# The first stage of an encoder layer, reordered: the first pair of row tiles, the first transform's cosine blocks, and the last tile's latents

## The chip, the cores and the metric

The kernel runs on one core of one Trainium2 chip. The metric is the device time of one execution in microseconds (us). Each version is run several times, and the median of the runs is its time.

## The reference

Two sequences (x_prompt and x_sample) of 1024 rows by 1024 columns in fp32 go through one layer, each with its own conditioning vector c:

```
mod = silu(c) @ w_ada + b_ada                     # six vectors of 1024
h   = rmsnorm(x, g_mix) * (1 + sc1) + sh1
z   = h @ w_in                                    # 256 q | 128 kv | 64 k_pe | 512 f_in
y_mla  = mla_group(z[q], z[kv], z[k_pe], ...)     # 4 heads, latents rms-normed, rotary k_pe
y_four = real(fft2(f_in, over rows and within 8 groups of 64 columns)) @ w_four
x = x + ga1 * (concat(y_mla, y_four) @ w_out)
h2 = rmsnorm(x, g_ffn) * (1 + sc2) + sh2
x = x + ga2 * ((silu(h2 @ w_gate) * (h2 @ w_up)) @ w_down)
return rmsnorm(x, g_final)
```

## The kernel before

Every fp32 operand of a large product is split into a high part (a cast on ScalarE) and a low part (a subtraction on VectorE), and each product is three matmuls (high·high, high·low, low·high; `mm3`, lines 78 to 80). The split is `split`, lines 62 and 63.

**Stage 1**, the first 230 us or so, works through eight pairs of row tiles, k = 0 to 7, four pairs for each sequence. A pair is two tiles (u = 0, 1) of 128 rows by 1024 columns; two rows of x that are mirror images in the sequence stand in the two tiles, so that the first Fourier product can use their sum ("even") and difference ("odd"). For a pair there is:

- `x_load(k)`: two transfers of 512 KB into the tiles `xt`, of which there are four, issued from SyncE (SP).
- `norm(k)`: the squares of each row on ScalarE (L354, tile `junk`), the reciprocal root on GpSimd (`rstd`, six small operations L101 to L108), and the scaling of both `xt` tiles in place on VectorE (L357). The reciprocal root is taken for both tiles together.
- `flip(k, g)`, g = 0 to 3: transposes of `xt` on TensorE (L370), the modulation on ScalarE (`hf`, L377), the split into `hh` and `hl`.
- `evenodd(k)`: GpSimd adds and subtracts the halves of `hf` (`eo`, L392), and each result is split into `eoh` and `eol`.
- `zproj(k, u)`: 24 matmuls 448 wide; then squares (L406, L407) on ScalarE, `rstd` on GpSimd, rotary products (L413 to L415, tile `t`) and their sum (L417, GpSimd), the scaled latents `lat` (L418, L419) on VectorE, the split `kv`, and its two stores to `ckv_d` (L424) from SP.
- `latents(k, u)`: four transposes of `lat` (L433), the split into `lh` and `ll`, two stores to `lat_d` (L438).
- `fourier_in(k, i)`: 24 matmuls with the even (i = 0, 280 wide) or odd (i = 1, 256 wide) half against the constant `wcs`, and the copy out (L448).

Beside the pairs a generator `extras()` is advanced three times in each pair. It computes the modulation vectors ga1 and ga2 with eight chunks of w_ada (two loads of 512 KB each into `wada`, of which there are two; L202), one chunk a step with four matmuls (L211), and then combines them with w_out in four groups (L299, stores `wm_d` and `wn_d`).

After stage 1, `dft(0)` applies the transform over the rows to the first sequence: per block q, a product with the cosines (`pe`, operand `zh`) and one with the rest (`po`; for its first chunk the operand is `zod`). Then follow the folding of weights, the output of the Fourier part, the second sequence, attention, the output projection and the FFN.

The order of the work is set by a scheduler that takes the program order as priority and its own estimates as times; `issue_after` and `first` add dependencies that only fix an order. Each engine then executes its list strictly in order. SP has one list: a transfer that waits for its data holds back every transfer behind it.

Of the kernel before, what the change touches and what calls it, by code (L numbers as in the profile page):

```python
# [21 lines left out]
P = 128  # L22
D = 1024
N = 1024
NC = D // P
# [27 lines left out]
def hybrid_encoder_kernel(ctx: ExitStack, tc: tile.TileContext, a: dict):  # L53
# [105 lines left out]
    with ExitStack() as st:  # L159
# [36 lines left out]
        def wada_tile():  # L196
            return w2.tile([P, 4, 512], F32, tag="wada", name="wada", bufs=2)
# [67 lines left out]
        def extras():  # L265


            cols1 = [(2 * D, D), (5 * D, D)]
            wt = mod_load(0, cols1, wada_tile())
            yield  # L270
            yield
            wo4 = []
            for c in range(NC):
                if c + 1 < NC:
                    nxt = mod_load(c + 1, cols1, wada_tile())
                else:
# [69 lines left out]
        def norm(k):  # L346
# [6 lines left out]
                jk = w.tile([P, D], BF16, tag="junk", name="junk", bufs=1)  # L353
                nc.scalar.activation(jk, t, AF.Square, scale=1.0 / 32.0, accum_out=ms[:, u : u + 1])  # L354
            r = rstd(ms, 2)
            for u in range(2):
                nc.vector.tensor_scalar(out=xt[u], in0=xt[u], scalar1=r[:, u : u + 1], scalar2=None, op0=ALU.mult)  # L357

        def flip(k, g):
            s, j = pairs[k]  # L360
# [20 lines left out]
        def evenodd(k, root=None):  # L381

            hf = st1.pop(("hf", k))
            eo = []
            for i, op in enumerate((ALU.add, ALU.subtract)):
                f = w.tile([P, NC, P], F32, tag="eo", name="eo", bufs=1)
                fh = w.tile([P, NC, P], F32R, tag=f"eoh{i}", name="eoh", bufs=1)
                fl = w.tile([P, NC, P], F32R, tag=f"eol{i}", name="eol", bufs=1)
                for g in range(2):
                    gs = slice(4 * g, 4 * g + 4)  # L390
                    with tc.issue_after(root) if root is not None and i == 1 else ExitStack():
                        nc.gpsimd.tensor_tensor(out=f[:, gs], in0=hf[:, gs, 0, :], in1=hf[:, gs, 1, :], op=op)  # L392
                    split(fh[:, gs], fl[:, gs], f[:, gs])
                eo.append((fh, fl))
            st1["eo", k] = eo

        def zproj(k, u):
            s, j = pairs[k]
# [3 lines left out]
            for c in range(NC):  # L402
# [4 lines left out]
            nc.scalar.activation(jk[:, QL : QL + KVL], pz[:, QL : QL + KVL], AF.Square, scale=1.0 / math.sqrt(KVL),  # L407
                                 accum_out=mz[:, 1:2])
# [6 lines left out]
            nc.vector.tensor_tensor(out=t1[:, 96:], in0=kp[:, :32], in1=ropes[:, ti, 32:], op=ALU.mult)  # L415
            for d in range(2):
                nc.gpsimd.tensor_tensor(out=sk[:, 384 + 64 * d : 448 + 64 * d], in0=t1[:, :64], in1=t1[:, 64:], op=ALU.add)  # L417
            nc.vector.tensor_scalar(out=sk[:, :QL], in0=pz[:, :QL], scalar1=rz[:, 0:1], scalar2=None, op0=ALU.mult)  # L418
            nc.vector.tensor_scalar(out=sk[:, QL : QL + KVL], in0=pz[:, QL : QL + KVL], scalar1=rz[:, 1:2],  # L419
                                    scalar2=None, op0=ALU.mult)  # L420
# [116 lines left out]
        x_load(2)  # L537
        with behind():
            norm(1)
        norm1 = here["p"]  # L540
        zproj(0, 0)
        evenodd(0, norm1)
        nk = len(pairs)
        more = extras()
# [174 lines left out]
    with ExitStack() as st:  # L719
# [39 lines left out]
        def dft(s):  # L759
            z, od = zh.pop(s)  # L760
            A = [w.tile([P, 2, NT], F32R, tag=f"A{i}", name=f"A{i}", bufs=1) for i in range(2)]
            B = [w.tile([P, 2, 512], F32R, tag=f"B{i}", name=f"B{i}", bufs=1) for i in range(2)]
            for q in (0, 2, 1) if s == 0 else (0, 1):
# [996 lines left out]
```

## Time and profile before

| | |
|---|---|
| runs | 2083.09, 2083.04, 2084.96 us; median 2083.09 us |
| profiled execution | 2080.3 us, of which the span of instructions is 2078.5 us |
| mean granted TensorE clock | 0.996 |
| PE (TensorE matmul) busy | 2025.1 us, 97% of the span |
| VectorE (DVE), ScalarE (ACT), GpSimd (POOL) busy | 1414.6, 902.0, 821.4 us |

The span runs from the first to the last instruction. A row of a timeline gives start, duration, engine, line, operation, the names of output and inputs, the number of instructions that were grouped, and in brackets the idle time of the engine just before and what ended it.

### The profile page before, as it was taken

How to read it: one execution, taken by the hardware profiler on the slowest of the kernel's cores; microseconds unless marked ns; L12 is line 12 of the kernel's file. 1: busy time of each engine (PE TensorE's matmuls, PEld its weight loads, DVE VectorE, ACT ScalarE, POOL GpSimd, SP SyncE). 2: the span in 40 equal slices, each digit the busy share in tenths (PEclk: the TensorE clock that was granted, in tenths of full speed). 3: DMA queues.
4: the chain of work that ended last, by engine and by line, in shares of the span. 5: the costliest groups of instructions: out<-in, count | busy, mean ns of one | idle time of the engine just before them, and what ended most of it. 6: DMA issues, size and time to landing. Idle time of an engine off the chain costs nothing.

```text
span 2078.5 us, 28811 instructions
## 1 busy us (share of the span) xinstructions
PE 2025.1 (97%) x10044; PEld 1659.8 (80%) x10044; DVE 1414.6 (68%) x2085; ACT 902.0 (43%) x1763; POOL 821.4 (40%) x1013
## 2 busy tenths in 40 slices
PE   6899999999999999999999999999999999999998
PEld 3688878888888877888888888877788888888876
DVE  4657757666677667867677666778765666667685
ACT  3666535555565564233323255454323233336441
POOL 0555111111313325878778510333554454420142
PEclk9999999999999999999999999999999999999999
DMA  9675885544644465546446487675322232258662
GB/s 388 217 241 178 270 308 180 134 91 102 167 102 129 146 247 178 191 159 217 170 159 217 147 275 259 213 243 181 120 104 101 96 108 102 87 173 276 229 227 94
DMA packets 185342, 375.49 MB, mean 181 GB/s; under 512 B 18764, under 2 KB 58444, under 8 KB 182124
## 3 DMA queue, kind: packets, MB, share of 16 engines
q1 hardware_dynamic: 167212, 318.06, 45.1%
q0 software_dynamic: 17984, 55.59, 9.0%
q8 instruction: 79, 1.29, 0.3%
q14 instruction: 67, 0.55, 0.1%
HBM read 259.47 MB, written 122.49 MB: 184 GB/s over the span
## 4 chain that ended last, share of the span: by engine, by line
PE 51%; DMA 3%; DVE 3%; issue 1%; POOL 1%; ACT 1%; SPq 1%; DVEq 0%; ACTq 0%; POOLq 0%
PE bank L80 17%; PE bank L79 17%; PE bank L78 17%; DVE wl L63 1%; DMA H<-s_d 1%; DMA val<-x_d 1%; DMA draw<-t_d 1%; DMA draw<-s_d 1%; DVE val L137 1%; POOL val L137 1%; ACT wh L62 0%; DVE val L1566 0%; DMA rgu<-in_wgu_dram 0%; DVE H L63 0%; SPq L1526 0%
## 5 line engine op out<-in xcount | busy, mean ns | idle before, releaser
L80 PE MATMUL bank<-H,wl 128*128 128x512 f32 x1232 | 491.1, 399 | 1.4 <-DVE wl L63 1.4
L78 PE MATMUL bank<-H,wh 128*128 128x512 f32 x1232 | 483.7, 393 | 4.7 <-DVE val L1446 2.1
L79 PE MATMUL bank<-H,wh 128*128 128x512 f32 x1232 | 485.5, 394 | 0.2 <-DVE H L63 0.2
L78 PEld LDWEIGHTS bank<-H,wh 128*128 128x128 f32 x1232 | 231.2, 188 | 61.7 <-DVE val L1446 3.4
L79 PEld LDWEIGHTS bank<-H,wh 128*128 128x128 f32 x1232 | 231.3, 188 | 60.6 <-DVE H L63 0.6
L80 PEld LDWEIGHTS bank<-H,wl 128*128 128x128 f32 x1232 | 231.3, 188 | 55.0 <-DVE wl L63 1.7
L63 DVE TENSOR_TENSOR wl<-draw,wh 128x512 fp32r<-128x512 f32 x286 | 201.2, 737 | 87.4 <-ACT wh L62 87.0
L137 DVE TENSOR_TENSOR val<-bank,val 128x512 f32<-128x512 f32 x200 | 136.6, 689 | 157.3 <-PE bank L80 153.8
L62 ACT CAST wh<-draw 128x512 fp32r<-128x512 f32 x286 | 168.6, 619 | 161.1 <-PE bank L79 82.1
L137 POOL TENSOR_TENSOR val<-val 128x512 f32<-128x512 f32 x58 | 84.2, 1460 | 367.8 <-DVE val L1540 189.3
L79 PE MATMUL bank<-wl,wh 128*128 128x512 f32 x572 | 223.9, 391 | 2.5 <-DVE wl L63 2.5
L78 PE MATMUL bank<-wh 128*128 128x512 f32 x572 | 222.7, 389 | 0.4 <-ACT wh L62 0.4
L80 PE MATMUL bank<-wh,wl 128*128 128x512 f32 x572 | 222.7, 389 | 0.0
L62 ACT CAST wh<-rgu 128x512 fp32r<-128x512 f32 x172 | 106.7, 621 | 266.4 <-PE bank L79 205.8
L62 ACT CAST wh<-val 128x512 fp32r<-128x512 f32 x133 | 82.0, 620 | 276.4 <-PE bank L79 252.8
L63 DVE TENSOR_TENSOR wl<-val,wh 128x512 fp32r<-128x512 f32 x133 | 137.1, 1032 | 82.4 <-ACT wh L62 82.2
L63 DVE TENSOR_TENSOR wl<-rgu,wh 128x512 fp32r<-128x512 f32 x172 | 166.9, 970 | 3.5 <-ACT wh L62 3.4
L134 POOL TENSOR_TENSOR val<-rgu 128x512 f32<-128x512 f32 x80 | 117.4, 1467 | 108.2 <-DMA rgu<-in_wgu_dram 104.5
L79 PEld LDWEIGHTS bank<-wl,wh 128*128 128x128 f32 x572 | 107.3, 188 | 28.4 <-DVE wl L63 6.3
L78 PEld LDWEIGHTS bank<-wh 128*128 128x128 f32 x572 | 107.4, 188 | 23.4 <-ACT wh L62 0.8
L80 PEld LDWEIGHTS bank<-wh,wl 128*128 128x128 f32 x572 | 107.4, 188 | 22.0
L1024 DVE TENSOR_REDUCE mx<-ps_s 128x1 f32<-128x1024 f32 x64 | 78.2, 1222 | 62.0 <-PE ps_s L1019 61.8
(356 smaller groups left out, 4119.1 us busy)
## 6 DMA issues: line engine op xcount, KB each, us to landing
rgu<-in_wgu_dram SPq DMA_DIRECT2D x86, 512.0 KB, 4.2
draw<-s_d SPq DMA_DIRECT2D x143, 256.0 KB, 3.9
s_d<-val POOLq DMA_DIRECT2D x88, 256.0 KB, 3.9
draw<-t_d SPq DMA_DIRECT2D x88, 256.0 KB, 4.3
s_d<-val SPq DMA_DIRECT2D x66, 256.0 KB, 3.6
draw<-in_w_down_dram SPq DMA_DIRECT2D x55, 256.0 KB, 4.6
wada<-in_w_ada_dram SPq DMA_DIRECT2D x11, 1024.0 KB, 8.6
xt<-in_x_dram SPq DMA_DIRECT2D x16, 512.0 KB, 7.8
```

The lines of the kernel that those rows point to most:

```text
L62: here["a"] = nc.scalar.copy(hi, src).ins
L63: here["v"] = nc.vector.tensor_tensor(out=lo, in0=src, in1=rd(hi), op=ALU.subtract).ins
L78: nc.tensor.matmul(out, lh, rh, start=first, stop=False, skip_group_check=cont)
L79: nc.tensor.matmul(out, lh, rl, start=False, stop=False, skip_group_check=cont)
L80: here["t"] = nc.tensor.matmul(out, ll, rh, start=False, stop=last, skip_group_check=cont).ins
L134: return eng.tensor_tensor(out=out, in0=x, in1=y, op=ALU.subtract).ins
L137: eng.tensor_tensor(out=out, in0=x, in1=y, op=ALU.add)
L1024: nc.vector.tensor_reduce(out=mx, in_=ps, axis=AX.X, op=ALU.max)
```

## The change

Four edits:

1. `extras()` loads two chunks of w_ada ahead instead of one, and starts before `zproj(0, 0)`. The product of a chunk comes one step earlier, and so does all that follows it in the generator.
2. In the first pair the rotary products go ahead of the scaling of the second pair's `xt`; the odd half of `evenodd(0)` goes behind the first tile's rotary sum (GpSimd) and its splits behind the second tile's squares; the second tile's scaled latents go behind those splits. On TensorE `fourier_in(0, 1)` goes ahead of `latents(0, 1)`.
3. In the last pair `latents(7, 1)` goes behind the last matmul of `fourier_in(7, 1)`.
4. `dft(0)` does the cosine products of blocks 0 and 1 before any of the other products.

The core of the diff:

```
             cols1 = [(2 * D, D), (5 * D, D)]
-            wt = mod_load(0, cols1, wada_tile())
-            yield
+            ahead = [mod_load(c, cols1, wada_tile()) for c in range(2)]
             yield
             wo4 = []
             for c in range(NC):
-                if c + 1 < NC:
-                    nxt = mod_load(c + 1, cols1, wada_tile())
-                else:
+                mod_mm(1, c, ahead.pop(0))
+                if c + 2 < NC:
+                    ahead.append(mod_load(c + 2, cols1, wada_tile()))
+                elif c + 2 == NC:
...
-                mod_mm(1, c, wt)
-                wt = nxt
                 yield
...
-                    with tc.issue_after(root) if root is not None and i == 1 else ExitStack():
+                    with tc.issue_after(here["root"]) if i == 1 else ExitStack(), tc.issue_after(here["pe"]) if i == 1 and k == 0 else ExitStack():
                         nc.gpsimd.tensor_tensor(out=f[:, gs], in0=hf[:, gs, 0, :], in1=hf[:, gs, 1, :], op=op)
-                    split(fh[:, gs], fl[:, gs], f[:, gs])
+                    with tc.issue_after(here["sq"]) if i == 1 and k == 0 else ExitStack():
+                        split(fh[:, gs], fl[:, gs], f[:, gs])
...
+        scaled = here["xn"]
+        more = extras()
+        next(more)
         zproj(0, 0)
-        evenodd(0, norm1)
+        root0, here["pe"] = here["p"], here["kpe"]
+        for i in scaled:
+            first(here["rope"], i)
+        eo0 = evenodd_steps(0)
+        next(eo0)
         def first_pair():
             zproj(0, 1)
+            here["root"] = root0
+            lats = here["lat"]
+            next(eo0)
+            for i in lats:
+                first(here["v"], i)
             fourier_in(0, 0)
...
-            latents(0, 1)
+            fourier_in(0, 1)
+            with tc.issue_after(here["t"]):
+                latents(0, 1)
             next(more, None)
-            fourier_in(0, 1)
...
             fourier_in(k, 0)
-            latents(k, 1)
+            if k + 1 < nk:
+                latents(k, 1)
             next(more, None)
             fourier_in(k, 1)
+            if k + 1 == nk:
+                with tc.issue_after(here["t"]):
+                    latents(k, 1)
...
+            if s == 0:
+                cosines(0)
+                cosines(1)
             for q in (0, 2, 1) if s == 0 else (0, 1):
...
-                pe, po = bank2(), bank2()
-                for c in range(4):
-                    zz = [(zn[i] if q == 2 else z[0][i][:, :, sl])[:, c, :] for i in range(2)]
-                    mm3(pe[:m, :NTE], zz[0], zz[1], tb[0][0][:, c, :NTE], tb[0][1][:, c, :NTE], c == 0, c == 3)
+                if q not in pes:
+                    cosines(q)
+                pe, po = pes.pop(q), bank2()
```

Line numbers behind the edits shift: L370 becomes L368, L433 becomes L437, L424 becomes L428, L438 becomes L442, L344 becomes L342.

TensorE in the first pair, from the transposes of the second pair's tiles on (L370 or L368), before:

```order
L370 MATMUL bank<-ident,xt 128x128 x8
L433 MATMUL bank<-ident,lat 128x128 x4
L370 MATMUL bank<-ident,xt 128x128 x8
L433 MATMUL bank<-ident,lat 128x128 x4
L211 MATMUL bank<-wada,scT 32x512 x4
L78 MATMUL bank<-wcs_h,eoh 128x256
L79 MATMUL bank<-wcs_l,eoh 128x256
L80 MATMUL bank<-wcs_h,eol 128x256
```

and now:

```order
L368 MATMUL bank<-ident,xt 128x128 x8
L211 MATMUL bank<-wada,scT 32x512 x2
L437 MATMUL bank<-ident,lat 128x128 x4
L368 MATMUL bank<-ident,xt 128x128 x2
L211 MATMUL bank<-wada,scT 32x512 x2
L368 MATMUL bank<-ident,xt 128x128 x6
L78 MATMUL bank<-wcs_h,eoh 128x256
L79 MATMUL bank<-wcs_l,eoh 128x256
L80 MATMUL bank<-wcs_h,eol 128x256
```

A chunk's product (L211) now stands in halves among the transposes of the tiles and inside the odd Fourier product, and the second tile's latents are no longer ahead of that product.

SP's list, around the load of the fourth pair (k = 3: `xt_924` and `xt_925` before, `xt_941` and `xt_942` now). `kv_826` and `kv_907` are the latents of the tiles u = 0 and u = 1 of the second pair (k = 1). Before:

```order
L438 DMA lat_d00_91<-lh_655 512x1x128
L438 DMA lat_d01_92<-ll_656 512x1x128
L438 DMA lat_d00_91<-lh_684 512x1x128
L438 DMA lat_d01_92<-ll_685 512x1x128
L202 DMA wada_690<-in_w_ada_dram 128x1024 x2
L202 DMA wada_835<-in_w_ada_dram 128x1024 x2
L344 DMA xt_924<-in_x0_dram 128x1024
L344 DMA xt_925<-in_x0_dram 128x1024
```

and now:

```order
L202 DMA wada_740<-in_w_ada_dram 128x1024 x2
L428 DMA ckv_d00_95<-kv_826 128x128
L428 DMA ckv_d01_96<-kv_826 128x128
L202 DMA wada_856<-in_w_ada_dram 128x1024 x2
L442 DMA lat_d00_91<-lh_917 512x1x128
L428 DMA ckv_d00_95<-kv_907 128x128
L428 DMA ckv_d01_96<-kv_907 128x128
L442 DMA lat_d01_92<-ll_918 512x1x128
L342 DMA xt_941<-in_x0_dram 128x1024
L342 DMA xt_942<-in_x0_dram 128x1024
```

The load of the fourth pair stood directly behind the chunk loads and ahead of all stores of the second pair; it now stands behind the stores of both tiles of the second pair.

SP's list around the load of the second tile of the last pair (k = 7: `xt_2109` before, `xt_2130` and `xt_2131` now). `kv_1982` and `kv_2022` are the latents of tile u = 0 of the sixth pair (k = 5), `kv_2096` those of its tile u = 1. Before:

```order
L438 DMA lat_d10_93<-lh_1834 512x1x128
L438 DMA lat_d11_94<-ll_1835 512x1x128
L293 DMA gah_1840<-ga_d_81 128x512
L293 DMA gah_1841<-ga_d_81 128x512
L458 DMA zo1_116<-zo_115 1x14x20
L424 DMA ckv_d10_97<-kv_1982 128x128
L424 DMA ckv_d11_98<-kv_1982 128x128
L344 DMA xt_2109<-in_x1_dram 128x1024
```

and now:

```order
L428 DMA ckv_d10_97<-kv_2022 128x128
L428 DMA ckv_d11_98<-kv_2022 128x128
L442 DMA lat_d10_93<-lh_2106 512x1x128
L442 DMA lat_d11_94<-ll_2107 512x1x128
L342 DMA xt_2130<-in_x1_dram 128x1024
L428 DMA ckv_d10_97<-kv_2096 128x128
L428 DMA ckv_d11_98<-kv_2096 128x128
L342 DMA xt_2131<-in_x1_dram 128x1024
L442 DMA lat_d10_93<-lh_2165 512x1x128
```

The second tile's load has gone from behind the stores of tile u = 0 to behind those of tile u = 1 of the same pair. In the same way the load of the second tile of the fifth pair (k = 4) now stands behind the stores of tile u = 1 of the third pair.

More of the change, by code (lines that the diff above doesn't have):

```diff
@@ L355, in norm @@
             r = rstd(ms, 2)
-            for u in range(2):
-                nc.vector.tensor_scalar(out=xt[u], in0=xt[u], scalar1=r[:, u : u + 1], scalar2=None, op0=ALU.mult)
+            here["xn"] = [nc.vector.tensor_scalar(out=xt[u], in0=xt[u], scalar1=r[:, u : u + 1], scalar2=None, op0=ALU.mult).ins
+                          for u in range(2)]
         def flip(k, g):
@@ L379, in flip, with evenodd_steps @@
             split(st1["hh", k][:, gs], st1["hl", k][:, gs], hf[:, gs])
[L381 removed]
+        def evenodd_steps(k):
             hf = st1.pop(("hf", k))
[L384 removed]
+            eo = st1["eo", k] = []
             for i, op in enumerate((ALU.add, ALU.subtract)):
@@ L390, in evenodd @@
                     gs = slice(4 * g, 4 * g + 4)
-                    with tc.issue_after(root) if root is not None and i == 1 else ExitStack():
+                    with tc.issue_after(here["root"]) if i == 1 else ExitStack(), tc.issue_after(here["pe"]) if i == 1 and k == 0 else ExitStack():
                         nc.gpsimd.tensor_tensor(out=f[:, gs], in0=hf[:, gs, 0, :], in1=hf[:, gs, 1, :], op=op)
-                    split(fh[:, gs], fl[:, gs], f[:, gs])
+                    with tc.issue_after(here["sq"]) if i == 1 and k == 0 else ExitStack():
+                        split(fh[:, gs], fl[:, gs], f[:, gs])
                 eo.append((fh, fl))
-            st1["eo", k] = eo
+                yield
+        def evenodd(k, root):
+            here["root"] = root
+            for _ in evenodd_steps(k):
+                pass
         def zproj(k, u):
@@ L414, in zproj @@
             nc.vector.tensor_tensor(out=t1[:, 64:96], in0=kp[:, 32:], in1=ropes[:, ti, :32], op=ALU.mult)
-            nc.vector.tensor_tensor(out=t1[:, 96:], in0=kp[:, :32], in1=ropes[:, ti, 32:], op=ALU.mult)
+            here["rope"] = nc.vector.tensor_tensor(out=t1[:, 96:], in0=kp[:, :32], in1=ropes[:, ti, 32:], op=ALU.mult).ins
             for d in range(2):
[L417 to L420, printed above, removed]
+                here["kpe"] = nc.gpsimd.tensor_tensor(out=sk[:, 384 + 64 * d : 448 + 64 * d], in0=t1[:, :64], in1=t1[:, 64:],
+                                                      op=ALU.add).ins
+            here["lat"] = [nc.vector.tensor_scalar(out=sk[:, sl], in0=pz[:, sl], scalar1=rz[:, i : i + 1], scalar2=None, op0=ALU.mult).ins
+                           for i, sl in enumerate((slice(0, QL), slice(QL, QL + KVL)))]
             kv = w.tile([P, 2, KVL], F32R, tag="kv", name="kv", bufs=2)
@@ L539, in hybrid_encoder_kernel @@
             norm(1)
-        norm1 = here["p"]
+        nk = len(pairs)
+        scaled = here["xn"]
+        more = extras()
+        next(more)
         zproj(0, 0)
-        evenodd(0, norm1)
-        nk = len(pairs)
-        more = extras()
+        root0, here["pe"] = here["p"], here["kpe"]
[3 more added lines that the diff above has]
+        next(eo0)
         def first_pair():
             zproj(0, 1)
+            here["root"] = root0
[3 more added lines that the diff above has]
+                first(here["v"], i)
             fourier_in(0, 0)
@@ L762, in dft, with cosines @@
             B = [w.tile([P, 2, 512], F32R, tag=f"B{i}", name=f"B{i}", bufs=1) for i in range(2)]
+            pes = {}
+            def cosines(q):
+                m = NY2 if q == 2 else P
+                sl = slice(P * q, P * q + P)
+                pe = pes[q] = bank2()
+                for c in range(4):
+                    zz = [(zn[i] if q == 2 else z[0][i][:, :, sl])[:, c, :] for i in range(2)]
+                    mm3(pe[:m, :NTE], zz[0], zz[1], tb[0][0][:, c, :NTE], tb[0][1][:, c, :NTE], c == 0, c == 3)
+            if s == 0:
+                cosines(0)
+                cosines(1)
             for q in (0, 2, 1) if s == 0 else (0, 1):
```

4 lines of the change are left out of this document (2 added, 2 removed).

## The prediction

> **What bounds the kernel now.** I read the page first, then the waits of TensorE (PE), then its timeline where the waits lie.
>
> ```profile
> span 2078.5 us, 28811 instructions
> PE 2025.1 (97%) x10044; PEld 1659.8 (80%) x10044; DVE 1414.6 (68%) x2085; ACT 902.0 (43%) x1763; POOL 821.4 (40%) x1013
> ```
>
> PE is busy for 97% of the span, so a new order can only move its 53 us of idle time and its clock. The windows say where they lie:
>
> ```profile
> 0.00:100.00 100.00, 75.30 (x428) 51.85 (x428) 53.38 (x117) 47.34 (x113) 30.23 (x68) 0.95 0.83 307
> 100.00:2078.00 1978.00, 1949.77 (x9620) 1607.98 (x9616) 1361.19 (x1969) 854.65 (x1651) 791.18 (x945) 1.00 0.53 174
> ```
>
> After the stretch and its length come PE's busy time and, behind the brackets, its granted clock. Of the idle time 24.7 us lie in the first 100 us, where the clock is also lower. The waits of PE that the edits touch (total, times, longest):
>
> ```profile
> PE bank L211 <- ACT lh L62: 5.1, 1, 5.1
> PE bank L433 <- DVE lat L418: 3.8, 4, 1.8
> PE bank L78 <- ACT zod L62: 1.0, 1, 1.0
> ```
>
> The third is at the start of `dft(0)`; the first and most of the second are in the first pair, as PE's timeline shows:
>
> ```profile
> 62.78 1.03 PE L370 MATMUL bank<-ident,xt 128*128 128x128 f32 x8
> 65.64 0.63 PE L433 MATMUL bank<-ident,lat 128*128 128x128 f32 x4 [1.83 <-DVE lat L418]
> ...
> 68.71 0.63 PE L433 MATMUL bank<-ident,lat 128*128 128x128 f32 x4 [1.57 <-DVE lat L418]
> 74.43 3.15 PE L211 MATMUL bank<-wada,scT 128*32 128x512 f32 x8 [5.08 <-ACT lh L62]
> ...
> 81.21 0.37 PE L78 MATMUL bank<-wz_h,hh 128*128 128x448 f32 x1
> ...
> 86.02 1.03 PE L370 MATMUL bank<-ident,xt 128*128 128x128 f32 x8
> 86.98 1.06 PE L211 MATMUL bank<-wada,scT 128*32 128x512 f32 x8
> ```
>
> From 62.78 to 86.02 PE does two groups of transposes of x (0.96 each, the distance from 86.02 to 86.98), two of latents (about 0.47 each, half as many), one chunk product (about 1.0), `fourier_in(0, 1)` (24 matmuls, about 2.9 at full clock) and `zproj(1, 0)` (86.02 - 81.21 = 4.8). That is 11.5 us of work in 23.2, so 11.7 us are lost: 8.5 in the three waits, the rest to the clock:
>
> ```profile
> 34.21 1.37 PE L211 MATMUL bank<-wide,scT 128*32 128x512 f32 x8 [2.33 <-DMA wide<-in_w_ada_dram]
> 36.00:40.00 4.00, 4.00 (x16) 2.21 (x16) 1.50 (x2) 2.00 (x5) 1.55 (x6) 0.72 1.01 421
> 62.00:70.00 8.00, 3.94 (x32) 3.28 (x30) 4.35 (x18) 3.91 (x12) 5.77 (x16) 1.00 0.06 16
> 76.00:78.00 2.00, 2.00 (x8) 0.49 (x3) 0.69 (x1) 2.00 (x4) 0.29 (x2) 0.50 1.16 351
> 78.00:80.00 2.00, 2.00 (x14) 2.00 (x14) 0.91 (x2) 0.05 (x1) 1.67 (x6) 0.70 0.95 316
> ```
>
> The waits of 1.83 and 1.57 us left the clock at 1.00 (62 to 70). The wait of 2.33 us at 34.21 was followed by a clock of 0.72 up to 40: some 6 us x 0.28 = 1.7 us. The wait of 5.08 us was followed by 0.50 up to 78 and 0.70 up to 80: 4 x 0.5 + 2 x 0.3 = 2.6 us.
>
> **The first pair: a gain of 7.7 us.** Two rows show why the first tile's latents come late:
>
> ```profile
> 61.55 1.66 POOL L392 TENSOR_TENSOR eo<-hf 128x512 f32<-128x512 f32 x1
> 65.01 0.48 DVE L418 TENSOR_SCALAR lat<-bank,rs_r 128x256 f32<-128x256 f32 x1 [2.63 <-POOL rs_r L108]
> ```
>
> An odd half of 1.66 us stands inside the chain of the reciprocal root on GpSimd, and the rotary products that feed the chain stand behind the scaling of xt. The edit puts both the other way round, so the latents come about 2.6 us earlier and the wait of 1.83 goes. The second tile's transposes go behind `fourier_in(0, 1)`, which is 2.9 us of work: the wait of 1.57 is covered. The wait of 5.08 is put down to ScalarE's `lh`, which that product does not read; what it does read is its chunk, and that was asked for only at 70.03, behind four stores that wait for the latents:
>
> ```profile
> 70.03 0.90 SPq L202 DMA_DIRECT2D wada<-in_w_ada_dram x2
> 78.46 1.37 SPq L344 DMA_DIRECT2D xt<-in_x_dram x2
> 180.38 0.35 SPq L344 DMA_DIRECT2D xt<-in_x_dram x1
> 208.14 0.80 SPq L424 DMA_DIRECT2D ckv_d<-kv x2
> ```
>
> Now it is asked for ahead of them, 15 us before its use, so the wait of 5.08 goes and with it 2.6 us of slow clock. What is late next: the odd half itself (about 0.3 us); the third chunk, whose buffer is free only after the first product, and which stands in SP's list behind the same stores: asked for near 69.6 it lands 4.4 us later (74.43 - 70.03), about 1.2 us after PE wants it; and the low part `hl`, queued on VectorE behind a scaling of xt, about 1.8 us. With 0.7 for clock, 4.0 of the 11.7 us stay lost. By the bounds, all of the new waits hidden but 2.2, the gain is 9.5; with a wait over 2.33 among them it is 5. The step earlier of the chunk products moves their 8 us, and does not change it.
>
> **The row transform and the last pair: a gain of 0.8 us.** The wait of 1.00 for `zod` falls behind twelve more matmuls, which cover it; the split that now stands ahead of the first product costs some 0.3 back, and the last latents' small wait goes. Bounds 0 and 1.4 us.
>
> **The late loads of x: a loss of 9.5 us.** The queue of SP is where the change costs. Three pairs' loads now stand behind the stores of tile u = 1 of the pair before last (fourth, fifth and last pair). When those stores are issued, and when PE wants the tile, come from pairs that ran undisturbed:
>
> ```profile
> 107.86 0.38 PE L370 MATMUL bank<-ident,xt 128*128 128x128 f32 x2
> ...
> 129.72 0.38 PE L370 MATMUL bank<-ident,xt 128*128 128x128 f32 x2
> ...
> 174.70 0.27 PE L370 MATMUL bank<-ident,xt 128*128 128x128 f32 x1
> ...
> 192.19 0.37 PE L78 MATMUL bank<-wz_h,hh 128*128 128x448 f32 x1
> ...
> 197.10 0.27 PE L370 MATMUL bank<-ident,xt 128*128 128x128 f32 x1
> ...
> 210.97 0.37 PE L78 MATMUL bank<-wz_h,hh 128*128 128x448 f32 x1
> ```
>
> From a pair's flips (F) to the next is 107.86 - 86.02 = 21.8 us, and 129.72 - 107.86 = 21.9 with three chunk products; two leave 20.8; with nothing of `extras` it is 210.97 - 192.19 = 18.8. The stores of u = 1 were issued at 208.14, 11.0 us after the flips at 197.10, and both were out at F + 11.9. Until now the load of the fourth pair was out at 78.46, before F (86.02), and the last at 180.38, 5.7 us after its F (174.70). From landing to flips:
>
> ```profile
> L354 ACT ACTIVATE junk<-xt x14: 1045/1057/1102, 54.6 to 188.8; 128x1024 bf16<-128x1024 f32 x14
> L354 ACT ACTIVATION_READ_ACCUMULATOR junk<-xt x14: 188/191/235, 55.6 to 189.7; 128x1 f32 x14
> ...
> DMA to landing us min/median/max: 4.6/6.2/7.8
> ```
>
> ```profile
> 77.63 0.22 POOL L101 TENSOR_SCALAR rs_v<-ms 128x2 f32<-128x2 f32 x1 [2.29 <-ACT junk L354]
> ...
> 79.55 0.20 POOL L108 TENSOR_TENSOR rs_r<-rs_w,rs_y 128x2 f32<-128x2 f32 x1
> ```
>
> ```profile
> 79.78 3.46 DVE L357 TENSOR_SCALAR xt<-xt,rs_r 128x1024 f32<-128x1024 f32 x2 [1.01 <-POOL rs_r L108]
> ...
> 192.22 0.75 DVE L357 TENSOR_SCALAR xt<-xt,rs_r 128x1024 f32<-128x1024 f32 x1
> ...
> 193.49 0.75 DVE L357 TENSOR_SCALAR xt<-xt,rs_r 128x1024 f32<-128x1024 f32 x1
> ```
>
> Squares 1.25, root 2.1 (77.63 to 79.75), scaling between 1.5 (two at 0.75) and 3.46; I take 2.4, and 2.0 in the last pair (192.22 to 194.24). The wait is then:
>
> - fourth pair: second load out at F + 13.1, behind one more store and its twin; landing after 6.2; ready at 13.1 + 6.2 + 5.8 = 25.1 against 21.8: 3.3 us (0.8 to 5.9 by the ends of landing and scaling).
> - fifth pair: out at F + 11.9; one load alone, so I take 5.4, between the least and the median landing; 11.9 + 5.4 + 5.8 = 23.1 against 20.8: 2.3 us (0.6 to 5.8).
> - last pair: 11.9 + 5.4 + 5.4 = 22.7 against 18.8: 3.9 us (2.6 to 7.8).
>
> PE's list has the flips ahead of `zproj` of the second tile, so nothing else runs in that wait, and PE has no slack later to give it back.
>
> **The clock behind these waits: a loss of 4.2 us.** Two waits are longer than 2.33 us and cost 1.7 each; the middle one is at the edge, 0.8. Bounds 1.7 (one) and 7.8 (three at 2.6). The Trainium skill, TensorE: Matmul & The Clock Gate, Part 1 (What's actually happening), has the clock halved only after an idle window of about 3.4 us; by it only the last wait would cost, about 1.7 in place of 4.2, and the sum would be 2.5 us lower. The row at 34.21 with 0.72 behind it speaks against it here.
>
> **The sum.** -7.7 - 0.8 + 9.5 + 4.2 = +5.2 us. The profiled execution took 2080.3 us, 1.8 more than its span and 2.8 less than the median of 2083.09, so 2085.5 us in such an execution and 2088.3 us as a median. About 0.2%, 4.2 us, is what a measurement of this kernel can tell from no change.
>
> **The rivals.**
>
> - *The late loads cost their least (faster).* Landing within 4.6 us and scaling in 1.5 leave waits of 0.8, 0.6 and 2.6, 4.0 in all; if the clock holds behind the 2.6, and the gains are at their best, that is -9.5 - 1.4 + 4.0 = -6.9, 2076.2 us (with the gains of 7.7 and 0.8 it is -4.5). It decides at a landing of about 5 us. For it: one load alone met 4.6. Against it: the median of 6.2 and 3.46 for the scaling beside GpSimd's work. The Trainium skill, DMA: Bandwidth & Descriptors (Anatomy of one DMA), has 2.0 us and 436 KB for each us, an estimate of 3.2 us for 512 KB, by which the waits would be 0.3, 0 and 1.7 and the result near 2076; no landing of xt in these rows is below 4.6.
> - *All three late and cold (slower).* Landing after 7.8, scaling in 3.46 and 2.6 us of slow clock each: 19.5 + 7.8 - 8.5 = +18.8, 2101.9 us. For it: 7.8 is what a pair of loads met beside chunk loads, which the fourth pair still does. Against it: the last pair's load has little beside it.
> - *The first pair gains little.* The new waits there (third chunk, `hl`) join into one of over 2.33 us and the clock falls, or the odd half comes later than reckoned, so that the reorder does not do what it says: a gain of 3 in place of 7.7, so +9.9, 2093.0 us. Against it: the largest wait, 5.08 us, has a plain cause that goes.
>
> **How the numbers follow.** Chances: forecast 0.45, least cost 0.25, all late 0.13, little gain 0.17. The forecast's own range is +0 to +10 us, with two fifths of it within 4.2. So slower: 0.26 of the forecast and 0.26 of the last two, less their edges, 0.50; within 0.2%: 0.18 + 0.06 = 0.24; faster 0.26. The range takes in the least-cost case at 2076 and stops short of the full price of all late, at 2099.
>
> **What would show it.** Right: the waits of PE for `lat` and `lh` in the first pair gone, the flips of the third pair near 80; waits at L368 for the scaled xt of the fourth, fifth and last pair, of 2 to 4 us, with ScalarE's squares waiting for the transfer and the clock at about 0.7 after them. Wrong: no wait at L368, or landings under 5 us; or PE still idle over 6 us between the first flips and 86 us.

## The result

The changed kernel takes 2092.68 us as a median of eight runs (2085.24 to 2097.61), the kernel before 2082.84 us (2079.55 to 2084.96). The ratio is 1.004, with a 95% interval of 1.0027 to 1.0052: slower by 0.4%, within the range that was given, and 4.4 us above the forecast. The profiled execution took 2094.89 us, with a span of 2093.1, 14.6 us over the span of before.

### The profile page after: what moved, and what is told of

Read it like the earlier page. It is cut to its first block, busy times and chain, and to the rows that moved or that the text cites. A ratio compares the mean times of both kernels' runs of the same rounds, so it can differ in the third digit from the quotient of the medians.

```text
span 2093.1 us, 28815 instructions
## 1 busy us (share of the span) xinstructions
PE 2036.4 (97%) x10044; PEld 1665.6 (80%) x10044; DVE 1418.2 (68%) x2085; ACT 903.0 (43%) x1763; POOL 825.5 (39%) x1013
## 4 chain that ended last, share of the span: by engine, by line
PE 52%; DVE 3%; DMA 3%; ACT 1%; issue 1%; POOL 1%; SPq 0%; DVEq 0%; ACTq 0%; POOLq 0%
PE bank L79 17%; PE bank L78 17%; PE bank L80 17%; DVE wl L63 1%; DMA rgu<-in_wgu_dram 1%; DMA H<-in_w_down_dram 1%; ACT wh L62 1%; DVE val L137 1%; DMA H<-s_d 1%; DVE val L1597 0%; DVE H L63 0%; POOL val L134 0%; DMA draw<-s_d 0%; DMA draw<-t_d 0%; DVE val L134 0%
## 5 line engine op out<-in xcount | busy, mean ns | idle before, releaser
L80 PE MATMUL bank<-H,wl 128*128 128x512 f32 x1232 | 484.4, 393 | 1.4 <-DVE wl L63 1.4
L80 PEld LDWEIGHTS bank<-H,wl 128*128 128x128 f32 x1232 | 231.3, 188 | 59.2 <-DVE wl L63 1.7
L80 PE MATMUL bank<-wh,wl 128*128 128x512 f32 x572 | 222.7, 389 | 0.0
L80 PEld LDWEIGHTS bank<-wh,wl 128*128 128x128 f32 x572 | 107.4, 188 | 21.9
```

Source lines behind the costliest of these rows:

```text
L80: here["t"] = nc.tensor.matmul(out, ll, rh, start=False, stop=last, skip_group_check=cont).ins
```

## The profile after

The page and the waits of PE in the changed kernel (total, times, longest):

```profile
span 2093.1 us, 28815 instructions
PE 2036.4 (97%) x10044; PEld 1665.6 (80%) x10044; DVE 1418.2 (68%) x2085; ACT 903.0 (43%) x1763; POOL 825.5 (39%) x1013
```

```profile
PE bank L368 <- DVE xt L354: 9.0, 6, 2.0
...
PE bank L437 <- POOL lat L421: 1.1, 1, 1.1
```

PE does the same 10044 matmuls, but it is busy for 11.3 us more: part of them ran at a lower clock, and some that stood side by side before now stand alone. The wait of 5.1 us at L211 and those of 3.4 us for the first pair's latents are gone; 9.0 us of waiting for a scaled xt are new. PE's timeline in the first pair:

```profile
64.94 1.03 PE L368 MATMUL bank<-ident,xt 128*128 128x128 f32 x8
65.90 1.05 PE L211 MATMUL bank<-wada,scT 128*32 128x512 f32 x4
66.88 0.66 PE L437 MATMUL bank<-ident,lat 128*128 128x128 f32 x4
...
81.00 0.47 PE L80 MATMUL bank<-wz_h,hl 128*128 128x448 f32 x1 [0.40 <-DVE hl L63]
...
83.10 1.03 PE L368 MATMUL bank<-ident,xt 128*128 128x128 f32 x8
```

From the second pair's first flips to the third pair's it is now 18.2 us instead of 23.2, and three chunk products are done in it instead of one. Hardly any wait is left. But see what a product costs: before, the eight instructions of a chunk (two for each of its four matmuls) took from 86.98 to 87.98, 1.0 us; here four of them, half a chunk, take from 65.90 to 66.88, 0.98 us. The four matmuls of a chunk write 32 rows of the output each, and together they cost what two cost. Three chunks in halves are 2.9 us of extra PE time in this stretch, and a fourth in the next pair is 1.0 more.

Then come the three late loads. PE's timeline at the flips of the fourth, fifth and last pair:

```profile
108.44 0.30 PE L368 MATMUL bank<-ident,xt 128*128 128x128 f32 x1 [2.01 <-DVE xt L354]
110.02 0.98 PE L368 MATMUL bank<-ident,xt 128*128 128x128 f32 x7 [1.28 <-DVE xt L354]
...
133.60 0.30 PE L368 MATMUL bank<-ident,xt 128*128 128x128 f32 x1 [1.23 <-DVE xt L354]
135.18 1.76 PE L368 MATMUL bank<-ident,xt 128*128 128x128 f32 x7 [1.28 <-DVE xt L354]
...
206.25 0.30 PE L368 MATMUL bank<-ident,xt 128*128 128x128 f32 x1 [1.86 <-DVE xt L354]
207.84 1.75 PE L368 MATMUL bank<-ident,xt 128*128 128x128 f32 x7 [1.29 <-DVE xt L354]
```

Each is two waits with one transpose between: for the first scaled tile, then for the second. SP's, ScalarE's, VectorE's and GpSimd's timelines show how the first of them comes about:

```profile
95.56 0.80 SPq L428 DMA_DIRECT2D ckv_d<-kv  x2
...
96.99 1.12 SPq L342 DMA_DIRECT2D xt<-in_x_dram  x2
```

```profile
101.75 1.06 ACT L352 ACTIVATE junk<-xt 128x1024 bf16<-128x1024 f32 x1 [2.82 <-DMA xt<-in_x_dram]
```

```profile
106.56 3.40 DVE L354 TENSOR_SCALAR xt<-xt,rs_r 128x1024 f32<-128x1024 f32 x2 [6.83 <-POOL rs_r L108]
```

```profile
106.48 2.93 POOL L390 TENSOR_TENSOR eo<-hf 128x512 f32<-128x512 f32 x2
```

The loads go out at 96.99, 13.9 us after the third pair's flips and right behind the stores; ScalarE stands idle for them; and the scaling takes 3.40 us, not 1.5, beside GpSimd's odd half. The granted clock (the number behind the brackets) after the three waits:

```profile
108.00:112.00 4.00, 2.28 (x16) 1.04 (x16) 3.50 (x7) 2.95 (x10) 2.54 (x3) 0.91 0.32 129
112.00:116.00 4.00, 4.00 (x16) 3.15 (x13) 2.14 (x5) 1.97 (x5) 2.58 (x8) 0.67 0.57 175
134.00:138.00 4.00, 2.82 (x11) 2.69 (x12) 2.66 (x6) 3.13 (x9) 2.30 (x6) 0.64 0.88 342
138.00:142.00 4.00, 4.00 (x20) 3.71 (x19) 2.78 (x5) 1.50 (x4) 2.08 (x5) 0.93 0.20 70
207.00:211.00 4.00, 3.16 (x12) 2.99 (x13) 2.32 (x6) 3.23 (x9) 2.22 (x8) 0.50 0.01 2
211.00:215.00 4.00, 4.00 (x16) 3.59 (x15) 2.76 (x5) 1.38 (x3) 1.79 (x3) 0.67 0.11 33
```

Each window's length times what its clock lacks of 1.00 gives 1.7, 1.7 and 3.3 us: 6.7 in all, in this execution. At the start of the row transform:

```profile
242.00 0.36 PE L78 MATMUL bank<-tb,zh 128*128 128x258 f32 x1 [1.49 <-DVE ll L63]
242.85 0.39 PE L80 MATMUL bank<-tb,zh 128*128 128x258 f32 x1 [0.25 <-DVE zh L63]
...
258.48 0.50 PE L78 MATMUL bank<-wm,B 128*128 128x512 f32 x1 [0.19 <-ACT B L62]
...
259.52 0.50 PE L80 MATMUL bank<-wm,B 128*128 128x512 f32 x1 [0.31 <-DVE B L63]
...
261.99 0.79 PE L80 MATMUL bank<-wm,B 128*128 128x512 f32 x1 [1.49 <-DVE B L63]
```

The same stretch of the kernel before, from the last latents on:

```profile
224.46 0.63 PE L433 MATMUL bank<-ident,lat 128*128 128x128 f32 x4 [0.15 <-DVE lat L418]
...
228.90 0.39 PE L78 MATMUL bank<-tb,zh 128*128 128x258 f32 x1 [0.98 <-ACT zh L62]
...
229.63 0.39 PE L80 MATMUL bank<-tb,zh 128*128 128x258 f32 x1 [0.22 <-DVE zh L63]
...
232.08 0.38 PE L78 MATMUL bank<-tb,zod 128*128 128x256 f32 x1 [1.00 <-ACT zod L62]
...
248.24 0.51 PE L80 MATMUL bank<-wm,B 128*128 128x512 f32 x1 [0.78 <-DVE B L63]
```

The wait for `zod` is gone, but the first product waits half a us longer, now for the low part of the latents, and B comes later.

**Where the 14.6 us are.** The second pair's flips begin at 64.94 instead of 62.78: 2.2 us of the difference lie ahead of the first changed instruction of PE. They belong to the execution, not to the change: the profiled executions of the kernels below, whose PE work up to there is that of before, begin these flips between 62.4 and 65.4. To keep this out, I measure **stage 1** from the second pair's first flips to the first product of the row transform: 228.90 - 62.78 = 166.1 us before, 242.00 - 64.94 = 177.1 us now, 11.0 us more. The remaining 1.5 us lie behind it.

## The experiments

Theory A is the prediction's: the late loads of x are the loss. Its rival, B, has the loss in the first pair, in the halved products or the reorder itself. "Stage 1" is the length just defined. It is read from one execution, and not always a typical one: that of "before, loads late" was the slowest of five (2102.81 us), that of "products at the old steps" the fastest of eleven (2077.76 us).

| kernel | median us | ratio to before, 95% | stage 1 us, one execution |
|---|---|---|---|
| changed | 2092.68 | 1.0027 to 1.0052 | 177.1 |
| changed, loads early | 2086.13 | 1.0003 to 1.0021 | 167.5 |
| before, loads late | 2095.03 | 1.0039 to 1.0067 | 179.5 |
| changed, first edit undone | 2084.03 | 0.9996 to 1.0014 | 166.7 |
| first edit alone | 2091.39 | 1.0022 to 1.0047 | 173.8 |
| third and fourth edit alone | 2083.99 | 0.9995 to 1.0012 | 166.6 |
| fourth edit alone | 2082.05 | 0.9985 to 1.0009 | 166.9 |
| changed, whole chunks | 2087.36 | 1.0009 to 1.0028 | 169.0 |
| changed, loads early, whole chunks | 2086.47 | 1.0005 to 1.0022 | 168.2 |
| the same, products at the old steps | 2082.42 | 0.9981 to 0.9999 | 163.9 |
| the same, third pair's norm early (a) | 2081.17 | 0.9977 to 0.9998 | 164.9 |
| the same (b) | 2081.51 | 0.9979 to 0.9997 | 164.0 |

### The changed kernel with early loads

```
         def pair(k):
...
+            if k + 2 < nk:
+                x_load(k + 2)
             zproj(k, 0)
...
-            if k + 2 < nk:
-                x_load(k + 2)
             next(more, None)
             fourier_in(k, 0)
```

> The changed kernel with one edit: the loads of x for the pair after next stand at the head of a pair's program instead of behind its transposes, so that SP issues them ahead of that pair's stores. Theory A (the late loads are the loss): the three waits for the scaled xt, 9.0 us in the trace of the changed kernel, and the slow clock behind them, 6.7 us, go: about 15 us under the changed kernel, 2077 us, faster than before by 6. One more chunk's product is now in halves, which may give back 1. Theory B (the loss lies elsewhere: in the halved chunk products, or in the start of the program): no change against the changed kernel, 2092.

2086.13 us: 6.5 us under the changed kernel, not 15, and still above before. In the trace all three waits for xt are gone, and stage 1 is 9.6 us shorter than in the changed kernel. A part was given back at once. PE's timeline has new waits, nearly all for latents:

```profile
135.54 0.63 PE L437 MATMUL bank<-ident,lat 128*128 128x128 f32 x4 [1.12 <-DVE lat L423]
...
159.58 0.52 PE L437 MATMUL bank<-ident,lat 128*128 128x128 f32 x3 [1.36 <-DVE lat L423]
161.24 0.33 PE L437 MATMUL bank<-ident,lat 128*128 128x128 f32 x1 [1.15 <-POOL lat L421]
...
205.61 0.63 PE L437 MATMUL bank<-ident,lat 128*128 128x128 f32 x4 [0.68 <-DVE lat L423]
...
211.08 0.63 PE L437 MATMUL bank<-ident,lat 128*128 128x128 f32 x4 [0.85 <-DVE lat L423]
```

5.2 us in all, where before had 0.4 behind the first pair. Beside them a fifth chunk product is in halves, and PE waits 0.5 us for a chunk. What makes them is in the timelines of PE, GpSimd and ScalarE ahead of the fourth:

```profile
198.99 1.03 PE L368 MATMUL bank<-ident,xt 128*128 128x128 f32 x8
```

```profile
198.93 2.52 POOL L390 TENSOR_TENSOR eo<-hf 128x512 f32<-128x512 f32 x2 [2.13 <-DVE eol L63]
```

```profile
201.49 0.62 ACT L62 CAST eoh<-eo 128x512 fp32r<-128x512 f32 x1 [0.63 <-POOL eo L390]
202.02 0.38 ACT L410 ACTIVATE junk<-bank 128x256 bf16<-128x256 f32 x1
```

PE was through with `zproj(6, 0)` and at the last pair's flips at 198.99, but ScalarE's squares of it (L410) stand in its list behind the split of the odd half, which waits for GpSimd. That chain (scaling, even split, odd half, odd split, squares, root, latents) takes its time whatever PE has to do beside it. The change has pulled the chunk products and groups one step forward, out of these pairs; PE gets to the latents sooner and waits.

### The kernel before with late loads

```
+        late = {3: (0, 1), 4: (1,), 7: (1,)}
...
             for u in range(2):
-                nc.sync.dma_start(st1["x", k][u], xs[s][rows(j, u), :])
+                with tc.issue_after(here["ck"]) if u in late.get(k, ()) else ExitStack():
+                    nc.sync.dma_start(st1["x", k][u], xs[s][rows(j, u), :])
...
-                nc.sync.dma_start(ckv_d[s][i][:, ti, :], rd(kv[:, i, :]))
+                here["ck"] = nc.sync.dma_start(ckv_d[s][i][:, ti, :], rd(kv[:, i, :])).ins
```

> The kernel before with one edit: the loads of x that stand late in the changed kernel (both tiles of the fourth pair, the second tile of the fifth and of the last) are put behind the stores of tile u = 1 of the pair before last. Nothing else of the change. Theory A: the same three waits appear, 7 to 10 us, and 5 to 7 us of slow clock: 2095 to 2099 us. Theory B: the waits are hidden, 2083 us.

2095.03 us, within what theory A expected. Its waits of PE:

```profile
PE bank L373 <- DVE xt L360: 8.3, 5, 2.9
```

Stage 1 is 13.4 us longer than before: 8.3 of waiting and about 5 of slow clock behind the waits at the fourth and the last pair. The late loads alone, with nothing else of the change, cost as much as the whole change does: 0.53% and 0.40%, with intervals that overlap. Put into the kernel before they cost 11 us, taken out of the changed kernel 6.5, so what they cost depends on the work beside them.

### The changed kernel with the first edit undone

The generator is that of before (one chunk ahead, started behind the first tiles); the other three edits stay.

```
-            ahead = [mod_load(c, cols1, wada_tile()) for c in range(2)]
+            wt = mod_load(0, cols1, wada_tile())
+            yield
             yield
...
-        more = extras()
-        next(more)
         zproj(0, 0)
...
         next(eo0)
+        more = extras()
```

> The changed kernel with the first edit undone: the chunks of w_ada are loaded one ahead and start after the first tiles, as before. SP's list then has the loads of x of the fourth, fifth and last pair early again. Theory A: none of the three waits, and of the first pair's gain all but the chunk's wait, which stays in part (the chunk lands at about 74.4, and the odd Fourier product can now run ahead of it): 2078 to 2081 us. Theory B: 2088 or more.

2084.03 us, not to be told from before, and worse than theory A had it by 3 to 6 us. The loads of x are early again, and PE waits at the flips for 1.4 us in all (the third pair). So the late loads come from the first edit, not from the reorder. And the other three edits together bring next to nothing: stage 1 is 0.5 us longer than before. Its waits of PE in the first pair:

```profile
PE bank L211 <- DMA wada<-in_w_ada_dram: 4.2, 6, 1.0
...
PE bank L80 <- DVE eol L63: 1.9, 1, 1.9
...
PE bank L370 <- DVE xt L356: 1.4, 2, 1.2
```

(Some 2 us of the first line lie in the first two pairs.) The odd half comes 1.9 us late for its product when the chunk products are not there to fill the time, and the third pair's scaling is the next thing that PE reaches too early. The stretch from the second pair's flips until PE reaches the third pair's is shorter, 19.2 us instead of 23.2, but the next one, to the fourth pair's, is 4.8 us longer. This kernel has split products too: the first and the fourth chunk in two parts, the second in three, each part 0.98 us, so PE has some 4 us more work. What the reorder alone would bring without them, no run here shows.

### The first edit alone

```
-            wt = mod_load(0, cols1, wada_tile())
-            yield
+            ahead = [mod_load(c, cols1, wada_tile()) for c in range(2)]
             yield
             wo4 = []
             for c in range(NC):
...
+        more = extras()
+        next(more)
         zproj(0, 0)
         evenodd(0, norm1)
```

> The kernel before with the first edit alone: two chunks ahead, products and groups a step earlier. SP's list has the loads of x of the fourth, fifth and last pair late, as in the changed kernel. Theory A (this edit holds the whole loss): waits for the scaled xt of 8 to 9 us with 6 us of slow clock, less the wait of 5 us for the first chunk: 2089 to 2094 us. Theory B (the reordering of the first pair makes the loads late): no such waits, 2079 us.

2091.39 us, theory A. The waits for xt are there:

```profile
PE bank L368 <- DVE xt L355: 8.2, 6, 2.1
```

With the run before, this settles it from both sides: the first edit alone holds nearly the whole loss (8 of 10 us), and the change without it has none. The first edit also splits four products and moves all of them a step; its loss is not divided further here than by the 6.5 and 11 us above.

### The third and fourth edit, and the fourth alone

The edits are those of the diff; in the second kernel the last tile's latents stay where they were.

> The kernel before with the third and fourth edit alone: the last tile's latents behind its Fourier product, and both cosine blocks ahead in the first row transform. As predicted: 0.8 us gained, 2083. By the trace of the changed kernel, where the first product of the transform waits 1.5 us for the low part of these latents and the next stage 1.5 us for B instead of 0.8: 0 to 1 us lost, 2084. Either is within what can be told from no change; the waits in the trace tell them apart.

> The kernel before with the fourth edit alone. If the latents are what delays the first product, its wait stays at 1.0 us for zh as before, and the wait of 1.0 us for zod goes: 2082 us.

2083.99 and 2082.05 us; by time neither can be told from before. The waits can be told apart. With both edits:

```profile
229.01 0.39 PE L78 MATMUL bank<-tb,zh 128*128 128x258 f32 x1 [1.19 <-ACT zh L62]
230.15 0.39 PE L80 MATMUL bank<-tb,zh 128*128 128x258 f32 x1 [0.51 <-DVE zh L63]
...
248.19 0.50 PE L80 MATMUL bank<-wm,B 128*128 128x512 f32 x1 [1.44 <-DVE B L63]
```

With the cosines alone:

```profile
232.23 0.39 PE L78 MATMUL bank<-tb,zh 128*128 128x258 f32 x1 [0.98 <-ACT zh L62]
...
250.28 0.51 PE L80 MATMUL bank<-wm,B 128*128 128x512 f32 x1 [0.68 <-DVE B L63]
```

The wait of 1.0 us for `zod` is gone in both. The cosines alone leave 1.7 us of waits in this stretch; with the latents moved it is 3.1, as much as before. The latents' split, which now stands right ahead of the transform's, takes back what the cosines give.

### Whole chunks

```
-            for j in range(4):
+            for j in ((2, 3, 0, 1) if key else range(4)):
```

> The changed kernel with one edit: a chunk's four matmuls in the order 2, 3, 0, 1, so that they stand together. Loads of x: the fourth pair's first tile stands one store pair earlier and the fifth pair's both early, the last pair's as late as in the changed kernel. If a halved chunk costs a whole one (0.98 us for two matmuls), four chunks give back 3.9 us of PE's work, less a wait of up to 5 us for the third chunk, as in the kernel with early loads; with one late load fewer, 2.5 us of waiting and 1.7 of clock less: 2085 to 2090 us. If halves cost nothing: 2088 to 2091.

> The changed kernel with early loads of x and one more edit: the four matmuls of a chunk are written in the order 2, 3, 0, 1, so that the pair whose transfer is issued last is first, and the four stand together. In the trace of the changed kernel two matmuls of a chunk take 0.98 us where four together took 1.0. Theory A with whole chunks: 4.9 us under the kernel with early loads alone (five halved chunks), 2072 us, and all four products at about 1.0. Rival: the halves fill time in which PE would wait for hl or the odd half anyway; then the gain is 0 to 2 us and new waits stand in the first pair.

2087.36 and 2086.47 us. In the second the expected 2072 is missed by far: it is no better than the kernel with early loads and halves. The rival holds by its time, though the new wait is for a chunk and not for `hl` or the odd half. PE's timeline of the one with early loads:

```profile
78.13 1.93 PE L211 MATMUL bank<-wada,scT 128*32 128x512 f32 x8 [5.17 <-DMA wada<-in_w_ada_dram]
```

The third chunk's transfer is asked for only when the first product has freed its buffer, behind the stores; with whole products PE reaches it 5.2 us early, waits, and its clock falls. In halves, by this reading, the products themselves filled that time. The changed kernel with whole chunks is 5 us faster than without, but its loads have moved too, and its waits for xt are 2.7 us instead of 9.0; so the price of the halves is not settled by its time:

```profile
PE bank L368 <- DVE xt L354: 2.7, 2, 1.4
```

### Products at the old steps, two chunks loaded early

The kernel with early loads and whole chunks, and in the generator:

```
             ahead = [mod_load(c, cols1, wada_tile()) for c in range(2)]
             yield
+            yield
+            yield
```

> The changed kernel with three edits: the loads of x at the head of a pair, a chunk's matmuls in the order 2, 3, 0, 1, and the products of the chunks at the steps where they were before (two chunks are still loaded ahead, early). Theory A, extended by what the kernel with early loads showed (pairs from which the groups were taken away wait for their latents, 5 us in all): no waits for xt, no wait of over 1.5 us for a chunk, the pairs padded as before: the first pair's gain stays, 2075 to 2079 us. Rival: the gain of the first pair is eaten by the chain over GpSimd in the pairs behind it however the products are placed: 2082 to 2085.

2082.42 us: faster than before by 0.1%, the interval (0.9981 to 0.9999) just clear of one. That is less than expected and within the rival's range. Stage 1 is 2.2 us shorter than before in the profiled execution. The waits for latents are down to 0.4 us, which bears out that the moved products had uncovered them. Two waits took the place of the first pair's gain:

```profile
67.62 0.39 PE L80 MATMUL bank<-wcs_h,eol 128*128 128x256 f32 x1 [1.85 <-DVE eol L63]
...
82.20 0.65 PE L370 MATMUL bank<-ident,xt 128*128 128x128 f32 x2 [2.62 <-DVE xt L356]
```

### The third pair's norm early, in two places

The kernel above with the last tile's latents back in their old place, and `norm(2)` moved from the end of the first pair to behind `latents(0, 0)` (a), or ahead of `fourier_in(0, 0)` (b):

```
             latents(0, 0)
+            norm(2)
+            root2 = here["p"]
...
-            norm(2)
-            evenodd(1, here["p"])
+            evenodd(1, root2)
```

> The kernel with early loads, whole chunks and products at their old steps, with two more edits: the norm of the third pair's tiles stands behind the first latents instead of at the end of the first pair, and the last tile's latents stand where they were before the change. In the kernel without these edits PE waited 2.6 us at the third pair's flips for the scaled xt, and the row transform's first products 1.2 and 0.5 us. Theory: the 2.6 us and about 1 us at the transform go; hh of the second pair comes up to 2.5 us later on ScalarE and takes part of it back: 2079 to 2081 us. Rival: what is late is the whole chain of ScalarE, and the wait moves to hh or lat at the same size: 2082.5.

> The same, with the norm of the third pair's tiles still earlier, ahead of the first Fourier product in the program; the squares then stand ahead of the second pair's second modulation on ScalarE and the root ahead of its even half on GpSimd. Theory: as above, 2079 to 2081 us, with the wait at hh rather than at xt. Rival: 2082.5 or more.

2081.17 and 2081.51 us, ratios of 0.9987 (0.9977 to 0.9998) and 0.9988 (0.9979 to 0.9997): the fastest kernels here, 0.1% under before, between what the theory and its rival expected. The wait at the flips is gone, but it has moved to `hl` of the second pair, 3.75 us in (b) and in (a):

```profile
81.89 0.74 PE L80 MATMUL bank<-wz_h,hl 128*128 128x448 f32 x1 [3.15 <-DVE hl L63]
```

So the rival has the mechanism. The 1 us between these medians and that of the kernel without the two edits is within the noise (the intervals overlap), and the profiled executions show no gain: stage 1 is 164.9 and 164.0 us, against 163.9. By this the first pair is bound by the work of ScalarE, GpSimd and VectorE, whichever of their results PE asks for first; that reading rests on where the wait went, no run takes work off these engines.

## Why the prediction was right, and where it was off

- **The late loads: right in kind, and the size in part by luck.** Predicted 3.3, 2.3 and 3.9 us, 9.5 in all; measured 3.3, 2.5 and 3.1, 9.0. Two errors cancelled. The landings took 5.4 and 4.6 us and about 4.2 (out at 196.79, ScalarE starts at 200.98), not 6.2, 5.4 and 5.4; but from the second tile's squares to its scaling done it took 6.8 us each time, not 5.8, 5.8 and 5.4. The step that was mis-sized is the scaling, taken at 2.4 and 2.0: it was 3.4 us in all three, and not by chance. The program orders GpSimd's odd half behind the same reciprocal root that the scaling waits for, so with a late root the two start together (at 106.48 and 106.56, 131.63 and 131.71, 204.30 and 204.38), and a late load makes its own scaling 1.9 us dearer. "Landings under 5 us" was named as a sign of being wrong; two of the three were, and the waits stood all the same. In the fourth pair PE also came 1.5 us later than reckoned, and the load went out later by about as much. That the late loads alone make the kernel slower is shown by putting them into the kernel before and by taking them out of the changed one.
- **The clock behind them: right in kind, too small.** Predicted 4.2, measured 6.7. The step that failed is "the middle one is at the edge, 0.8": all three lowered the clock, also the 2.5 us in two parts, and the last cost 3.3. By the rule of the Trainium skill (TensorE: Matmul & The Clock Gate, Part 1), none of the three would have, each single wait being under 3.4 us; the rows of this kernel speak against taking it as a threshold. Nor is there another length in these runs that decides: a wait of 1.85 us at the same matmul of the first pair (L80 for `eol`) brought the clock down to about 0.50 in three executions (first edit undone, products at the old steps, third pair's norm early (a)) and left it at 1.00 in a fourth (b), and the pair of waits of 1.07 and 1.28 us in the first edit alone left it at 1.00. So the 6.7 us are those of one execution, and what decides stays open.
- **The first pair: right in size, not in its steps.** Predicted 7.7; measured 5.1 in the stretch and two more chunk products done, worth 2.0: 7.1. That the wait of 5.08 us was for the chunk, as predicted, is borne out by the kernels with the late loads and with the cosines alone, where the same wait of 5.3 us is put down to that transfer. But the waits that were to stay (1.2 for the third chunk, 1.8 for `hl`) shrank to 0.4, because, by this reading, three products in halves took 2.9 us more of PE and filled them. "The step earlier of the chunk products moves their 8 us, and does not change it" was the wrong step: a halved product costs a whole one more, and the fourth, in the next pair, was 1.0 us without cover.
- **What the moved products uncovered: missed.** The prediction said that moving them changes nothing. In the changed kernel there is one new wait of 1.1 us (L437 for `lat`); with early loads it was 5.2 us, so the late loads hid the rest.
- **The row transform and the last pair: wrong in sign, and outside its bounds.** Predicted 0.8 gained, between 0 and 1.4; 0.6 were lost. The waits were 3.1 us before (0.15 and 0.98 and 0.22 and 1.00 and 0.78) and 3.7 in the changed kernel (1.49 and 0.25 and 0.19 and 0.31 and 1.49). The step that failed is the price of the split that stands ahead, 0.3: by the kernels with both edits and with the cosines alone it is 0.7 at the first products (1.70 against 0.98) and 0.8 more at B (1.44 against 0.68).
- **The sum.** -7.1 + 1.0 + 9.0 + 6.7 + 1.1 + 0.6 = +11.3 by these terms, of which 0.2 lie behind stage 1; stage 1 is 11.0 longer. The forecast was +5.2. The difference is the clock (2.5), the transform (1.4), the latents (1.1), the fourth halved product (1.0) and 0.6 of the first pair, less 0.5 of the loads. The medians differ by 9.8.
- **The rivals.** The least-cost case did not come about: two landings were as short as it asks, but the scaling took 3.4 us beside GpSimd's odd half. The estimate of 3.2 us for a landing, after the Trainium skill, DMA: Bandwidth & Descriptors (Anatomy of one DMA), goes by a fit for transfers that GpSimd starts. These are started by SP, and the three took 4.2 to 5.4 us. The rival by which the first pair gains little, with a chance of 0.17, has 2093.0 us, and 2092.7 was measured: that is chance, for in the changed kernel the first pair gained 7.1, not 3, and the rest of the loss lies in the terms above.

What stays open: the start of the program varies by 3 us between executions, with the clock in the first 60 us (0.91 in the changed kernel's profile, 0.97 in that of before), and 1.5 us of the profiled difference lie behind stage 1. No run here was made to tell these apart.

## What to carry to other kernels

When a change moves work in a program that a scheduler orders, read the queue of the transfers first: moving the load of one tensor forward put three loads of another behind stores, and that cost more than the waits it removed. Before taking work out of a stage because another stage waits, ask what it was covering there: a stage whose other engines' chain is as long as PE's work may give nothing back when PE's work shrinks. And two orders that differ only in what stands between four small matmuls can differ by the whole price of the matmuls.

## What the runs showed of the hardware that was not expected

- Two of the four matmuls of a chunk product (128 x 32 weights, 512 wide) take 0.98 us, four together 1.0 us, and one alone 0.98 (86.72 to 87.70 in the kernel with the first edit undone, a row of two instructions): those that write different 32 rows run side by side when they stand together, and not across other matmuls.
- The granted clock fell after waits far shorter than the 5.08 us of before: after one of 1.86 us (first edit undone: 0.73, 0.50 and 0.92 in the windows of 2 us from 70 on), and after 1.23 and 1.28 us with one transpose between (changed kernel: 0.64 from 134 to 138). It did not fall after waits of 1.83 and 1.57 us in the kernel before, nor after 1.40 and 1.28 us with whole chunks (1.00 from 198 to 206). What decides between these is not shown.
- The price of a fall came in equal pieces. In the changed kernel the windows of 2 us from 110 on have 0.81, 0.50 and 0.83, a loss of 2 x (0.19 + 0.50 + 0.17) = 1.7 us, and those from 206 on have 0.71, 0.50, 0.50 and 0.59, a loss of 3.4; the fall in the kernel with the first edit undone comes to 1.7 too.
- The scaling of two tiles on VectorE took 3.40 us beside GpSimd's additions, and 1.4 to 1.5 us with GpSimd idle.
